# Decoder trunk: last two inner column tiles by rows, a join queued behind the first half's hi part, last products in halves

## The chip, the cores and the metric

One Trainium2 chip, one of its cores. The time is the device time of one execution in microseconds (us), the median over runs. Before the change it is 1212.53 us (three runs, 1212.32 to 1212.62).

The core's engines are named as in the profile: PE (TensorE, matrix products), PEld (its weight load), ACT (ScalarE), DVE (VectorE), POOL (GpSimd) and SP (SyncE, which issues most DMAs here). "t" is the token block: 256 tokens are two blocks of 128, t=0 and t=1.

## What is computed

Two layers, each of three residual steps with a layer norm behind it; the change touches the two feed-forward steps (four in all, at `i` = 0 and 2) and every layer norm.

```python
def _swiglu(x, w1, w3, w2):
    return (jax.nn.silu(x @ w1) * (x @ w3)) @ w2
...
for l in range(DEPTH):                                   # DEPTH = 2
    h = _swiglu(x, ffn_w1[l, 0], ffn_w3[l, 0], ffn_w2[l, 0])
    x = _layernorm(ALPHA * x + 0.5 * h, ln_g[l, 0], ln_b[l, 0])
    h = _mixer(x, l, ...)                                # projections, gating unit, attention, merge
    x = _layernorm(ALPHA * x + h, ln_g[l, 1], ln_b[l, 1])
    h = _swiglu(x, ffn_w1[l, 1], ffn_w3[l, 1], ffn_w2[l, 1])
    x = _layernorm(ALPHA * x + 0.5 * h, ln_g[l, 2], ln_b[l, 2])
```

x is 256 x 1024 in float32, the inner width of a feed-forward step is 2816 = 22 tiles of 128 columns.

## The kernel before

**Arithmetic.** Every float32 operand is split into a hi part (rounded to the PE's fp32r type by an ACT copy) and a lo part (source minus hi, by DVE). A product is three matmuls: hi x hi, lo x hi and hi x lo. All weights stream in as 1 MB pieces `raw` (ring of 4) by SP, are split by ACT and DVE into `whi` and `wlo` (rings of 8 each), and are used once.

**First feed-forward matrix.** Inner tiles 0 to 19 are five blocks of four tiles, computed *by rows*: x is the stationary operand, 512 weight columns move, and each block's two products (w1 and w3) land in a PSUM bank with tokens on partitions (`gemm_first`, `gemm_b2`, `gemm_rows`). `front` takes SiLU on ACT, the product with the w3 bank on DVE, writes the result as two 16-bit planes (`planes`, ACT), and SP turns them with two DMA transposes per block (L704). `columns` (L681 to L693) joins the turned planes on ACT and splits the result for the second matrix. Inner tiles 20 and 21 are computed *by columns* in `gemm_a2` (L275 to L302): the weights are stationary; for each of four weight tiles eight matmuls of 512 columns move x hi and x lo together (L283), then, for each tile, eight matmuls of 256 columns bring in the weights' lo part (L290). Each tile then takes one ACT copy (L291) and one DVE addition (L293), and each pair SiLU and a product (L721, L722). The result comes out inner-width first and needs no turning.

**Second feed-forward matrix.** Tiles 4 to 13 go through five rounds of a seven-product scheme (`SQ`, `stream_s`); the pairs 0-1, 2-3 and 14 to 21 are plain products (`PQ`). After the first round comes the first plain pair, after the second round the second, then the rounds go on alone. The last four plain pairs are *held* until the end, so that the four output blocks (t, c), c being the 512-column half, finish one after the other and the layer norm of t=0 can begin while PE is still at t=1.

**Layer norm into the next step** (`Norm`). `part_s` adds a finished block to the residual on DVE and accumulates its sum, `finish_s` takes the sum of squares on ACT (L553), the reciprocal root on DVE and normalises 512 columns at a time (L556). The second 512 columns go through planes (L184) and a DMA transpose (`send`); the first 512 are turned by PE (L633). `turn(t, h)` then brings half h of the normalised rows to the stationary form of the next step: for h = 0 out of PSUM, for h = 1 by a *join* of the turned planes (ACT, L628), then four ACT operations with scale and shift (L638), the hi part on ACT and the lo part on DVE (`split`, L233 and L234). The next step's PE work starts with t=0, c=0, for which half h = 0 must be there. Weight splits of the next step run on ACT and DVE at the same time (L174, L178, L207, L216, L227, L229).

**The last norm** (`part`, `finish`) has no next step: each block is added to the residual on DVE (L567), its statistics taken per 256 columns (L572), and for the last token block the columns below 768 are multiplied by the gain (L574) and finished through PE (L588, L592), the last 256 on DVE; six DMAs write the result.

**Order of work.** PE's order is the order in which the program is written, with turns of side tasks slotted in by a running beat counter. The other engines' order is set by a list scheduler when the program is built: by priority (`soon()` raises it by two chunks) among what its model of the time calls ready. `behind(ins)` queues an instruction after `ins` on the same engine and adds no wait of its own. Each engine's queue runs strictly in that order on the chip.

Of the kernel before, what the change touches and what calls it, by code (L numbers as in the profile page):

```python
# [58 lines left out]
def trunk(ctx, tc, x, xT, w13a, w13b, w2s, w2p, wb, wqk, wa, wbr, wo, gateb, sgug, sgub, sguwT, sgubias, lam, diffg,  # L59
# [89 lines left out]
    latest, added, emptied, silu, turned_by, early = [None, None], [None], [None], [None], [None], [None]  # L149
# [5 lines left out]
    def stream(src, width=CH, sub=HC, lent=(), after=(None, None)):  # L155
# [7 lines left out]
        for o in range(0, width, HC):  # L163
# [7 lines left out]
            for p, (h, w) in zip(range(0, HC, sub), at):  # L171
                r = raw[:, o + p : o + p + sub]
                with behind(latest[0] if o // HC in lent else early[0] or latest[0]):
                    copied = A.activation(h, r, AF.Copy)  # L174
                if o // HC in lent:
                    early[0] = copied.ins
                with behind(after[o // HC] or latest[1]):
                    V.tensor_tensor(out=w, in0=r, in1=h.bitcast(F32), op=ALU.subtract)  # L178
# [330 lines left out]
    class Norm:  # L509
# [6 lines left out]
        def __init__(self, l, i, scale, eps, after, last=False):  # L516
            self.scale, self.eps, self.last, self.done = scale, eps, last, set()
            self.ends, self.xlo, self.pre, self.sent = [None] * NT, {}, None, {}
# [103 lines left out]
        def turn(self, t, h):  # L622
            self.done.add((t, h))
            xf = s512("xf")
            if h:
                b = xf
                with soon():
                    A.activation(xf.bitcast(U16).rearrange("p (k w) -> p k w", w=2),  # L628
                                 self.sent[t].rearrange("p (w k) -> p k w", w=2), AF.Copy)
            else:  # L630
                b = side_bank()
                for k in range(4):
                    PE.transpose(b[:, k * P : (k + 1) * P], self.y[t][:, k * P : (k + 1) * P], ident)  # L633
# [7 lines left out]
            self.xlo[t, h] = last[1]  # L641
# [9 lines left out]
    def ffn(l, f, i, norm, following=None):  # L651
# [29 lines left out]
        def columns(ins):  # L681
            while waiting:
                k0, tt = waiting.pop(0)
                h = tmp.tile([P, 2, 512], F32, tag="columns", name=name("columns"), bufs=1)
                to = h.bitcast(U16).rearrange("p q (k u t w) -> p (q k) u t w", k=2, u=2, w=2)
                for t in range(NT):
                    with behind(ins):
                        A.activation(to[:, :, t], tt[:, t].bitcast(U16).rearrange("p (w c t) -> p c t w", w=2, c=FB),
                                     AF.Copy)
                for j in range(2):  # L690
# [19 lines left out]

        if norm is None:
# [28 lines left out]
        for n, q in enumerate(SQ):  # L740
# [4 lines left out]
            if n < len(PQ) - HELD:  # L745
                plain_pair(n)
        u, v = s512("u"), s512("v")
# [13 lines left out]
        for t in range(NT):  # L761
            for c in range(2):
                for ps, o, n in ends[t, c]:
                    for q in PQ[-HELD:]:
                        rows_p(ps, t, q, held[q, c], hh, hl, o, n, stop=q == PQ[-1])
                    if not last:
                        ln.part_s(t, c, ps)
                        continue
                    for o in ((0, 256) if last and (t, c) == (1, 1) else (0,)):
                        ln.part(t, c * 512 + o, ps[:, o : o + 256] if o or last and (t, c) == (1, 1) else ps, 1.0)  # L770
# [244 lines left out]
def _layout(i):  # L1015
# [32 lines left out]
    o["w13a"] = c(np.stack([cols(w1[..., nb:]), cols(w3[..., nb:])], axis=4)).reshape(L, 2, FT - FR, P, CH)  # L1048
# [52 lines left out]
```

## Time and profile before

| | us |
|---|---|
| median of 3 runs | 1212.53 (1212.32 to 1212.62) |
| profiled execution, its own time | 1213.05 |
| span of its instructions | 1211.3 |
| PE busy | 1203.7 (99% of the span) |
| PEld / DVE / ACT / POOL busy | 1011.3 / 942.9 / 857.4 / 91.1 |
| granted PE clock | 1.00 |
| DMA | 212 GB/s mean |

How to read it: an engine's rows are instructions with start and duration in us from the span's start. A matmul's duration is modelled and overlaps the next one, so PE's pace is read from starts: a run of n matmuls in the chain of waits has n times the spacing. "x2" in a row means two instructions merged in one row. In brackets stands the idle time before an instruction and what ended it.

### The profile page before, as it was taken

How to read it: one execution, taken by the hardware profiler on the slowest of the kernel's cores; microseconds unless marked ns; L12 is line 12 of the kernel's file. 1: busy time of each engine (PE TensorE's matmuls, PEld its weight loads, DVE VectorE, ACT ScalarE, POOL GpSimd, SP SyncE). 2: the span in 40 equal slices, each digit the busy share in tenths (PEclk: the TensorE clock that was granted, in tenths of full speed). 3: DMA queues.
4: the chain of work that ended last, by engine and by line, in shares of the span. 5: the costliest groups of instructions: out<-in, count | busy, mean ns of one | idle time of the engine just before them, and what ended most of it. 6: DMA issues, size and time to landing. Idle time of an engine off the chain costs nothing.

```text
span 1211.3 us, 16542 instructions
## 1 busy us (share of the span) xinstructions
PE 1203.7 (99%) x5961; PEld 1011.3 (83%) x5961; DVE 942.9 (78%) x1540; ACT 857.4 (71%) x1384; POOL 91.1 (8%) x184
## 2 busy tenths in 40 slices
PE   9999999999999999999999999999999999999998
PEld 8888888888888878888888888888888888888886
DVE  6658998885696876579985679989766877757797
ACT  7677677679865595776776776776898556867761
POOL 0100000233300000000000000003331000000000
PEclk9999999999999999999999999999999999999999
DMA  8985665655764658665668665766648456677551
GB/s 321 323 261 174 211 249 208 227 177 166 232 227 164 217 178 282 191 192 218 229 216 270 195 176 207 254 223 199 213 139 273 176 174 217 201 259 210 184 202 47
DMA packets 101346, 257.00 MB, mean 212 GB/s; under 512 B 66528, under 2 KB 67600, under 8 KB 74640
## 3 DMA queue, kind: packets, MB, share of 16 engines
q1 hardware_dynamic: 97296, 243.03, 59.9%
q0 software_dynamic: 3536, 12.13, 3.2%
q8 instruction: 46, 0.75, 0.3%
q10 hardware_dynamic: 432, 0.79, 0.2%
q14 instruction: 36, 0.29, 0.1%
HBM read 235.47 MB, written 1.05 MB: 195 GB/s over the span
## 4 chain that ended last, share of the span: by engine, by line
PE 91%; DVE 4%; ACT 3%; issue 1%; DMA 0%; SPq 0%; POOL 0%; DVEq 0%; ACTq 0%; POOLq 0%
PE bank L271 35%; PE sbank L271 24%; PE bank L283 16%; PE bank L290 8%; PE sbank L283 2%; PE bank L446 2%; PE sbank L290 1%; PE sbank L829 1%; DVE wlo L178 1%; PE sbank L961 1%; ACT pp L839 0%; DVE nwa L248 0%; ACT xf L638 0%; ACT whi L174 0%; PE sbank L878 0%
## 5 line engine op out<-in xcount | busy, mean ns | idle before, releaser
L178 DVE TENSOR_TENSOR wlo<-raw,whi 128x1024 fp32r<-128x1024 f32 (+1 forms) x396 | 436.6, 1125 | 144.5 <-ACT whi L174 113.9
L174 ACT ACTIVATE whi<-raw 128x1024 fp32r<-128x1024 f32 (+1 forms) x396 | 372.9, 971 | 124.4 <-PE bank L283 43.2
L271 PE MATMUL bank<-whi,x 128*128 128x512 f32 x840 | 263.3, 390 | 0.0
L271 PEld LDWEIGHTS bank<-whi,x 128*128 128x128 f32 x840 | 157.7, 188 | 32.9 <-DVE gz L293 0.2
L271 PE MATMUL bank<-wlo,x 128*128 128x512 f32 x420 | 163.5, 389 | 0.0
L271 PE MATMUL sbank<-whi,x 128*128 128x512 f32 x512 | 158.9, 389 | 0.0
L283 PE MATMUL bank<-x,whi 128*128 128x512 f32 x640 | 156.0, 394 | 0.0
L283 PEld LDWEIGHTS bank<-x,whi 128*128 128x128 f32 x640 | 117.1, 188 | 26.3 <-issue 2.3
L271 PEld LDWEIGHTS sbank<-whi,x 128*128 128x128 f32 x512 | 96.1, 188 | 20.0
L353 ACT ACTIVATE shi<-raw 128x1024 fp32r<-128x1024 f32 (+1 forms) x80 | 73.4, 946 | 51.7 <-DVE raw L368 26.4
L271 PE MATMUL sbank<-wlo,x 128*128 128x512 f32 x256 | 99.6, 389 | 0.0
L355 DVE TENSOR_TENSOR slo<-raw,shi 128x1024 fp32r<-128x1024 f32 (+1 forms) x80 | 85.4, 1088 | 14.1 <-ACT shi L353 13.3
L271 PEld LDWEIGHTS bank<-wlo,x 128*128 128x128 f32 x420 | 78.9, 188 | 16.0
L290 PE MATMUL bank<-x,wlo 128*128 128x256 f32 x640 | 85.9, 285 | 0.0
L290 PEld LDWEIGHTS bank<-x,wlo 128*128 128x128 f32 x640 | 81.6, 191 | 2.2
L291 ACT ACTIVATE r<-bank 128x256 f32<-128x256 f32 x112 | 41.6, 377 | 24.0 <-PE bank L290 24.0
L271 PEld LDWEIGHTS sbank<-wlo,x 128*128 128x128 f32 x256 | 48.1, 188 | 9.9
L271 PE MATMUL sbank<-whi,hhi 128*128 128x512 f32 x144 | 56.3, 391 | 0.0
L271 PE MATMUL sbank<-whi,hlo 128*128 128x512 f32 x144 | 56.1, 390 | 0.0
L271 PE MATMUL sbank<-wlo,hhi 128*128 128x512 f32 x144 | 56.0, 389 | 0.0
L506 POOL DMA_DIRECT2D bc<-in_lng x6 | 3.2, 530 | 696.2 <-DVE bc L505 696.2
L702 ACT ACTIVATE planes<-silu 128x1024 uint16<-128x1024 uint16 x40 | 42.0, 1053 | 7.3 <-DVE silu L701 6.2
(247 smaller groups left out, 1999.1 us busy)
## 6 DMA issues: line engine op xcount, KB each, us to landing
raw<-in_w13b SPq DMA_DIRECT2D x76, 1024.0 KB, 5.4
raw<-in_w2p SPq DMA_DIRECT2D x24, 1024.0 KB, 4.9
raw<-in_wa SPq DMA_DIRECT2D x24, 1024.0 KB, 5.4
raw<-in_w2s SPq DMA_DIRECT2D x20, 1024.0 KB, 4.9
raw<-in_wb SPq DMA_DIRECT2D x16, 1024.0 KB, 5.3
raw<-in_wqk SPq DMA_DIRECT2D x16, 1024.0 KB, 4.8
raw<-in_wbr SPq DMA_DIRECT2D x16, 1024.0 KB, 4.9
raw<-in_w13a SPq DMA_DIRECT2D x8, 1024.0 KB, 4.8
```

Of the source, the lines that this page charges most:

```text
L174: copied = A.activation(h, r, AF.Copy)
L178: V.tensor_tensor(out=w, in0=r, in1=h.bitcast(F32), op=ALU.subtract)
L271: PE.matmul(ps, xx, w, start=start and n == 0, stop=stop and n == 2)
L283: PE.matmul(b[-1], hi[:, k * P : (k + 1) * P], xc(k), start=k == 0, stop=False)
L290: PE.matmul(b[n][:, :T], lo[:, k * P : (k + 1) * P], xc(k)[:, :T], start=False, stop=k == KT - 1)
L291: emptied[0] = A.activation(r[:, s], b[n][:, T:], AF.Copy, scale=scale).ins
L353: A.activation(h, r, AF.Copy)
L355: V.tensor_tensor(out=w, in0=r, in1=h.bitcast(F32), op=ALU.subtract)
L446: PE.matmul(ps[t][m], x[:, j, o + t * P : o + (t + 1) * P], y, start=k0 + j == 0 and o == 0 and y is hi, stop=k0 + j == KT - 1 and y is lo)
L702: A.activation(pk.rearrange("p (w k) -> p w k", w=2), s.bitcast(U16).rearrange("p (k w) -> p w k", w=2), AF.Copy)
L829: PE.matmul(banks[m][:, j * nk : (j + 1) * nk], rows(qT, m, j, t * P, P), rows(kT, m, j, 0, nk), start=True, stop=True)
L961: PE.matmul(b[:, j * T + t * P : j * T + (t + 1) * P], vg[t][:, g // 4, s], wsT[g // 4][:, s], start=True, stop=True)
```

## The change

Three parts:

1. Tiles 20 and 21 are computed by rows too (`narrow`): w1 and w3 of both tiles are one 512-wide moving operand, two banks, one per t, each with w1 in its first and w3 in its second 256 columns. SiLU, product, planes and a DMA transpose follow per t, at half of `front`'s width. The join and split of the block before (`columns`) come after t=1's SiLU; those of the two tiles come after the second plain pair's weight split (`copied`). The weights' layout in memory follows.
2. In `turn`, the join of half h = 1 is queued behind the hi part of half h = 0 of the same t.
3. In the last feed-forward step the last output block, (t, c) = (1, 1), is multiplied in two halves of 256 columns. The first half adds on to the block's bank; the second has a new bank of its own, and what the old bank has for it is added to the residual on DVE while PE works at the second half. The first half's addition, statistics and gain come ahead of the second half's end.

```diff
@@ turn
-                with soon():
+                with soon(), behind(self.xhi[t]):
                     A.activation(xf.bitcast(U16).rearrange("p (k w) -> p k w", w=2),
                                  self.sent[t].rearrange("p (w k) -> p k w", w=2), AF.Copy)
...
-            self.xlo[t, h] = last[1]
+            self.xhi[t], self.xlo[t, h] = last
@@ ffn
+        def narrow():
+
+            tt = act.tile([P, 2, 512], F32, tag="val", name=name("turned"), bufs=2)
+            ps = [side_bank() for _ in range(NT)]
+            for c in range(2):
+                for n, piece in enumerate(stream(w13a[l, f, :, c * CH : (c + 1) * CH])):
+                    for t in range(NT):
+                        rows_b(ps[t], t, 4 * c + 2 * n, piece, xh, xl, KT)
+            for t in range(NT):
+                s, pk = t512("silu"), s512("planes")[:, :T].bitcast(U16)
+                silu[0] = A.activation(s[:, :T], ps[t][:, :T], AF.Silu).ins
+                V.tensor_tensor(out=s[:, :T], in0=s[:, :T], in1=ps[t][:, T:], op=ALU.mult)
+                planes(pk, s[:, :T])
+                nc.sync.dma_start_transpose(out=tt[:, t, :T].bitcast(U16).rearrange("p (c t) -> p c t", c=4), in_=pk)
+            columns(silu[0])
+            waiting.append((FR, tt))
+            return s
...
-        for j in range(FR, FT, 2):
-            qa = s512("qa")
-            for m, z in gemm_a2([w13a[l, f, j - FR + m] for m in range(2)], both, lambda m: t512("silu"), bank=side_bank):
-                s = z[:, :T]
-                silu[0] = A.activation(s, s, AF.Silu).ins
-                V.tensor_tensor(out=qa[:, m * T : (m + 1) * T], in0=s, in1=z[:, T:], op=ALU.mult)
-                columns(silu[0])
-            keep((j, j + 1), qa)
-        ln = Norm(l, i, 2.0 * ALPHA, 4.0 * EPS, qa[:, :1], last)
+        s = narrow()
+        ln = Norm(l, i, 2.0 * ALPHA, 4.0 * EPS, s[:, :1], last)
...
             if n < len(PQ) - HELD:
                 plain_pair(n)
+            if n == len(PQ) - HELD - 1:
+                columns(copied[0])
...
-                for ps, o, n in ends[t, c]:
...
+                (ps, _, _), = ends[t, c]
+                if last and (t, c) == (1, 1):
+                    y, right = ln.y[t][:, 768:], bank()
+                    for b, o, opens in ((ps, 0, False), (right, 256, True)):
+                        for q in PQ[-HELD:]:
+                            rows_p(b[:, :T], t, q, held[q, c], hh, hl, o, 256, stop=q == PQ[-1],
+                                   start=opens and q == PQ[-HELD])
+                        ln.part(t, 512 + o, b[:, :T], 1.0)
+                        if not opens:
+                            V.tensor_tensor(out=y, in0=y, in1=ps[:, T:], op=ALU.add)
+                    continue
```

`columns` takes a block of two tiles as well (`nq`: one pair and half the planes instead of two pairs), and `stream` notes its last hi copy in `copied`.

More of the change, by code (lines that the diff above doesn't have):

```diff
@@ L762, in ffn @@
             for c in range(2):
-                for ps, o, n in ends[t, c]:
[L764 to L770, printed above, removed]
+                (ps, _, _), = ends[t, c]
[9 more added lines that the diff above has]
+                    continue
+                for q in PQ[-HELD:]:
+                    rows_p(ps, t, q, held[q, c], hh, hl, 0, 512, stop=q == PQ[-1])
+                if last:
+                    ln.part(t, c * 512, ps, 1.0)
+                else:
+                    ln.part_s(t, c, ps)
             (ln.finish if last else ln.finish_s)(t, ((2, 1.5), (2, 1))[t])
```

20 lines of the change are left out of this document (11 added, 9 removed).

## The prediction

> **What bounds the kernel now.** I read the page first: where the span goes, and which engine carries the chain that ended last.
>
> ```profile
> span 1211.3 us, 16542 instructions
> ...
> PE 1203.7 (99%) x5961; PEld 1011.3 (83%) x5961; DVE 942.9 (78%) x1540; ACT 857.4 (71%) x1384; POOL 91.1 (8%) x184
> ...
> PE 91%; DVE 4%; ACT 3%; issue 1%; DMA 0%; SPq 0%; POOL 0%; DVEq 0%; ACTq 0%; POOLq 0%
> ```
>
> PE is the bound nearly everywhere. Time can only come from three places: cheaper matmuls, the few spots where PE waits, and the tail behind the last matmul. So I read the chain of waits next, in order of time, for the pace of PE around the columns that change form.
>
> ```profile
> 92.98 21.76 PE bank L271 x96
> 114.74 7.25 PE sbank L283 x32
> 121.99 3.83 PE sbank L290 x32
> 125.82 2.75 PE bank L271 x12
> ```
>
> Columns: start, duration, what. A block by rows is 96 matmuls of 512 columns in 21.76 us, 0.2267 us each. The column form starts exactly when the block before it ends (92.98 + 21.76 = 114.74), so nothing is waited for there; its 32 matmuls of 256 columns take 3.83 us, 0.1197 each, more than half of 0.2267. Then the waits, PE's alone: total, times, longest.
>
> ```profile
> PE sbank L633 <- DVE xtok L556: 0.8, 2, 0.4
> PE bank L271 <- DVE x L234: 0.5, 3, 0.2
> ```
>
> These two are the norm transitions: three times PE waits for the lo part of the first normed half, twice for rows to turn. There are five transitions: the three times are those out of a feed-forward step, the two those out of a mixer.
>
> **Part 1, tiles 20 and 21 by rows.** Removed per feed-forward step: 32 x 512 and 32 x 256 columns, 7.25 + 3.83 = 11.08 us, and 0.03 of restart behind it (2.75 against 12 x 0.2267 = 2.72). Added: 8 k-tiles x 2 token blocks x 3 matmuls = 48 of 512 columns, 48 x 0.2267 = 10.88 us. The columns streamed are the same; what goes is the surplus of the short matmuls. Saving 0.23 per step, 0.92 over four; low end 0.2 each, 0.8.
>
> The Trainium skill speaks against a surplus of this size: its page "TensorE: Matmul & The Clock Gate", section "Back-to-back issue gap", gives an isolated warm gap of N/2.4 + 2.5 ns, so 109 ns for 256 columns and 216 for 512; by that a split costs 2.5 ns per extra matmul, part 1 would give an estimated 0.04 per step, part 3 would cost 0.06, and the sum below would be 2.7 instead of 3.1. The trace disagrees, with 119.7 and 226.7 ns.
>
> On the other engines: four ACT copies and four DVE additions of 256 columns go, four in number on each; two planes operations, two joins at half width and two DMA transposes per step come. The block before has the same kind of work at full width inside a 21.76 us stage in which PE never waits, so I cost it at nothing. Queues: SP now has two transposes that wait for the planes, and the next weight load stands behind them if the scheduler puts it there; ACT has two joins and a hi split behind the second plain pair's weight split, with the third round's splits queued behind. Who would suffer is DVE, which is full there:
>
> ```profile
> 146.25:160.53 14.28, 14.28 (x64) 11.83 (x64) 14.00 (x15) 9.68 (x11) 0.00 (x0) 1.00 0.55 197
> ```
>
> In this stretch (PE, PEld, DVE, ACT) DVE works 14.00 of 14.28 us. But the change takes four additions off it shortly before, so it enters the stretch ahead rather than behind. Part 1: -0.92.
>
> **Part 2, the join behind the hi part.** First a transition out of a feed-forward step: PE, ACT, DVE (start, duration, instruction).
>
> ```profile
> 182.87 0.39 PE L271 MATMUL bank<-llo,x 128*128 128x512 f32 x1
> 183.44 0.73 PE L271 MATMUL bank<-lhi,x 128*128 128x512 f32 x2 [0.18 <-DVE x L234]
> 184.01 0.39 PE L271 MATMUL bank<-llo,x 128*128 128x512 f32 x1
> ...
> 189.92 0.60 PE L633 MATMUL sbank<-ident,xtok 128*128 128x128 f32 x4
> ```
> ```profile
> 179.38 1.49 ACT L638 ACTIVATE xf<-sbank,ln_b,ln_g 128x128 f32<-128x128 f32 x4
> 180.76 1.19 ACT L628 ACTIVATE xf<-sent 128x1024 uint16<-128x1024 uint16 x1
> 181.84 0.63 ACT L233 ACTIVATE x<-xf 128x512 fp32r<-128x512 f32 x1
> ```
> ```profile
> 182.09 0.69 DVE L178 TENSOR_TENSOR wlo<-raw,whi 128x512 fp32r<-128x512 f32 x1
> 182.69 0.69 DVE L234 TENSOR_TENSOR x<-xf,x 128x512 fp32r<-128x512 f32 x1
> ...
> 188.48 1.00 DVE L556 TENSOR_SCALAR xtok<-xtok,mv,nwy 128x512 f32<-128x512 f32 x2
> ```
>
> From 182.87 to 184.01 PE starts three matmuls, 0.68 at its pace; it takes 1.14, so 0.46 is lost. It waits for the lo part (182.69 + 0.69 = 183.38), which stands on DVE right behind a weight split, and for whose hi part (181.84) ACT first ran the join of the other half (180.76, to the next start 1.08). With the join behind it the hi part comes 1.08 earlier or, if the scheduler puts a weight split of about 0.5 into the freed slot, about 0.55 earlier; in both cases it is there before 182.09, and the lo part can have the weight split's slot: it ends at 182.78, PE needs it at 182.87 + 0.23 = 183.10, and the wait is gone. Behind `behind` nothing else waits: the join and the half that hangs on it come at most 0.5 to 1.1 later, and PE needs that half only 24 matmuls, 5.4 us, after the first. DVE's queue order is fixed when the program is built, so the gain needs the scheduler to see the hi part earlier too; a hi part earlier by one ACT operation should move the lo part by at least one DVE operation, since it has priority. Next late are PE's transposes of t=1 (189.92): their rows are normalised at 188.48 + 1.00 = 189.48, and 0.46 earlier PE would stand there at 189.46 and wait a little. I take 0.40 of 0.46, three times: 1.20; ends 0 and 3 x 0.46 = 1.38.
>
> Out of a mixer the same order does something else:
>
> ```profile
> 426.14 0.50 PE L271 MATMUL bank<-lhi,x 128*128 128x512 f32 x1
> ...
> 427.44 0.39 PE L271 MATMUL bank<-llo,x 128*128 128x512 f32 x1
> ...
> 433.89 0.66 PE L633 MATMUL sbank<-ident,xtok 128*128 128x128 f32 x4 [0.39 <-DVE xtok L556]
> ```
> ```profile
> 424.38 1.18 ACT L628 ACTIVATE xf<-sent 128x1024 uint16<-128x1024 uint16 x1
> 425.46 0.63 ACT L233 ACTIVATE x<-xf 128x512 fp32r<-128x512 f32 x1
> ...
> 428.56 1.14 ACT L553 ACTIVATE sq<-xtok,mv 128x1024 bf16<-128x1024 f32 x1
> ```
> ```profile
> 426.12 0.69 DVE L234 TENSOR_TENSOR x<-xf,x 128x512 fp32r<-128x512 f32 x1 [2.05 <-ACT x L233]
> ```
>
> Here DVE itself stood idle 2.05 us for the hi part, so the lo part surely comes earlier, and the 0.39 that PE loses from 426.14 to 427.44 (1.30 for four matmuls, 0.91 at pace) goes. But PE then only arrives earlier at the transposes (433.89), for which it waits 0.39 already and which hang on t=1's sum of squares (ACT, 428.56). That operation has no idle in front of it: it comes when ACT's queue comes to it. If it stays at 428.56, the gain is 0. If the scheduler, seeing the lo part and so the sums earlier, puts it ahead of one ACT operation of 0.5 us, the gain is 0.5, at most 0.39 + 0.39 = 0.78. If one more weight split gets in front of it, 0.5 is lost. Both ends lie close; I take 0.25, twice: 0.50; ends -1.0 and 1.56.
>
> **Part 3, the last block in halves.** DVE behind the last matmul:
>
> ```profile
> 1203.13 0.75 DVE L567 TENSOR_TENSOR xtok<-xtok,sbank 128x256 f32<-128x256 f32 x2 [2.38 <-PE sbank L271]
> 1203.80 0.74 DVE L572 BATCH_NORM_STATS2 st<-xtok 128x6 f32<-128x256 f32 x2
> 1204.46 0.41 DVE L574 TENSOR_TENSOR xtok<-xtok,bc 128x256 f32<-128x256 f32 x1
> 1204.78 0.26 DVE L579 BATCH_NORM_AGGREGATE mv<-st 128x2 f32<-128x24 f32 x1
> ```
>
> Between the first addition (1203.13) and the aggregate (1204.78) lie five operations in 1.65 us, 0.33 each. Three of them, the first half's addition, statistics and gain, move under the second half's matmuls (24 x 0.1197 = 2.9 us; with the new addition of the old bank's rest four operations, 1.3 us, so they are hidden). Left are two that depend on each other, so rather 0.41 to 0.45 each than 0.33: 0.9. Saved 0.75, at most 0.99. Added on PE: 48 x 0.1197 - 24 x 0.2267 = 0.30, wholly on the path. Net 0.45; ends 0.15 (if two new banks and the changed order cost PE as much again, 0.3) and 0.75. Everything behind the aggregate keeps its length.
>
> **The sum.** 0.92 + 1.20 + 0.50 + 0.45 = 3.07. The profiled execution's own time, 1213.05 (span 1211.3 and 1.75 around it), becomes 1209.98. It lies 0.52 above the median of the runs, 1212.53, and I take the runs' scale: 1212.53 - 3.07 = 1209.46, rounded 1209.5. What a measurement of this kernel can tell from no change is about 0.2%, 2.4 us: faster begins below 1210.1.
>
> **Rivals.** *The lo part stays where it is on DVE.* The weight split at 182.09 keeps its slot because the scheduler's time for the hi part is still later. Then the 1.20 fails and 0.92 + 0.50 + 0.45 = 1.87 is left: 1210.7, no measurable change. For it: DVE ran without a gap ahead of 182.69, so nothing on the chip forces a new order. Against: the three waits look alike, so one order decides all three, and the lo part has priority. Chance 0.22.
>
> *The later join costs as much as the earlier hi part gives,* at the mixers above all: the sum of squares slips by one ACT operation, 0.5 each, and 0.92 + 1.20 - 1.0 + 0.45 = 1.57 is left: 1211.0, no measurable change. For it: 428.56 has no slack. Against: its input comes earlier with the lo part, so it can as well move forward. Chance 0.15, small misses of several terms included.
>
> *Slower: SP's new transposes hold a weight load back.*
>
> ```profile
> 116.06 2.60 SPq L704 DMA_TRANSPOSE turned<-planes  x2
> ```
> ```profile
> 126.08 0.34 SPq L344 DMA_DIRECT2D raw<-in_w2s  x1
> ```
>
> The planes of the two tiles are there, by an estimate of SiLU, product and planes at 0.4 to 0.5 each (256 columns took 0.41 at L574), about 1.5 us after the two tiles' matmuls end at 125.8, at 127.3. If the load now at 126.08 is queued behind their two transposes (up to 2.60, as at 116.06), it goes at about 130. DVE in the rounds behind has 14.28 - 14.00 = 0.28 us to spare plus the 1.3 of four removed additions; from 1.6 us of starvation on, every further one is a us of PE, four times. At 3 us it is 4 x 1.4 = 5.6 against 3.07: 1215.1. For it: SP's queue is in order, and DVE is full there. Against: the full-width transposes at 116.06 stand in the same place of the block before and PE did not wait. Chance 0.06.
>
> **How the numbers follow.** The forecast has 0.57. Faster is the forecast alone, 0.57; the two middle rivals are no change, 0.37; the last is slower, 0.06. The range goes from 0.92 + 1.38 + 1.56 + 0.75 = 4.6 saved, rarely all at once, so 1207.9, to the middle rivals with the low ends of parts 1 and 3 (0.8 + 0 - 0.5 + 0.15 = 0.45), 1212.1.
>
> **What the changed profile would show.** Part 1: behind the last full block 48 matmuls of 512 columns in 10.88 us, at L271, and the next round starting 0.23 earlier. Part 2: no wait of PE for L234, 0.57 between two starts gone at three places; ACT with the hi part ahead of the join at all five; at the mixers the sum of squares tells which way it went. Part 3: the aggregate 0.9 behind the last addition's start. I am wrong if the three waits stand, if PE waits anew in the rounds behind the two tiles (L353 or L355 as what ended it), or if the transposes out of the mixers come later than now.

## The result and the profile after

The changed kernel takes 1219.26 us (median of 6 runs, 1217.05 to 1222.44) against 1212.70 (6 runs, 1212.32 to 1213.84). The ratio is 1.0053, 95% interval [1.0043, 1.0064]; the ratios here are taken over all runs, so they are not quite the quotients of the medians beside them. It is slower by 0.5%, where 0.3% faster was forecast. Its profiled execution took 1222.44 us, the longest of the six and 9.4 more than the one of before, so what the profile shows place by place adds up to more than the 6.6 us between the medians. One execution each of e2, e3 and e10 below was a slow one (2018.92, 6922.22 and 2092.35 us) and is left out of the numbers given for them.

From the page of the changed kernel, the span, the engines' busy time and the chain by engine:

```profile
span 1220.7 us, 16437 instructions
...
PE 1207.2 (99%) x5921; PEld 1010.9 (83%) x5921; DVE 937.9 (77%) x1525; ACT 861.2 (71%) x1384; POOL 90.2 (7%) x184
...
PE 62%; issue 20%; ACT 6%; DVE 6%; DMA 3%; POOL 2%; SPq 1%; DVEq 0%; POOLq 0%; ACTq 0%
```

PE stays 99% busy, since a matmul that is issued late is still counted. The chain tells more, but its shares have to be read with care: PE's falls from 91% to 62%, yet most of what it loses are two stretches of "issue", 77.23 and 135.75 us long, that end at 1014 and 1154 us. There the trail goes back along POOL's queue, which is idle ahead of the DMA issues of the norm's gain (`bc<-in_lng`), while PE works on. What counts is that such a DMA has entered the chain in the last feed-forward step. The chain of waits at the columns that changed form:

```profile
93.17 21.76 PE bank L272 x96
114.93 10.88 PE sbank L272 x48
125.81 2.72 PE bank L272 x12
```

10.88 us against 7.25 + 3.83, and the next round without a restart: part 1 does on PE what it promised. The waits of PE (total, times, longest):

```profile
PE sbank L853 <- ACT aT L889: 2.3, 2, 1.1
PE sbank L634 <- DVE xtok L557: 1.8, 3, 0.8
PE bank L272 <- DVE slo L356: 1.7, 2, 0.9
PE sbank L887 <- DVE pp L872: 1.6, 2, 1.3
```

The wait for the lo part (L234, now L235) is gone, as forecast. Three that were not there have come: two in attention (L853, L887), one in the rounds (`slo`, L356). Differences of the same matmuls' starts in the two traces say where the 9.40 us of span came from:

| place | us |
|---|---|
| first feed-forward step, its rounds included | +0.28 |
| transitions out of three feed-forward steps | +0.38, -0.28, -0.22 |
| attention of layer 0, of layer 1 | +1.87, +3.87 |
| rows in the second, third and fourth step | -0.20, -0.15, -0.24 |
| rounds of the fourth step | +4.46 |
| last block and tail | -0.38 |
| the two transitions out of a mixer | 0 |

**The rounds of the last step.** The changed kernel's DVE, then its ACT, then ACT of the kernel before, in order of time:

```profile
1156.25 0.69 DVE L235 TENSOR_TENSOR hlo<-columns,hhi 128x512 fp32r<-128x512 f32 x1 [2.45 <-ACT hhi L234]
1158.29 0.69 DVE L235 TENSOR_TENSOR hlo<-columns,hhi 128x512 fp32r<-128x512 f32 x1 [1.34 <-ACT hhi L234]
1161.01 2.36 DVE L356 TENSOR_TENSOR slo<-raw,shi 128x1024 fp32r<-128x1024 f32 x2 [2.03 <-ACT shi L354]
```
```profile
1156.24 1.28 ACT L532 ACT_TABLE_LOAD   x1
1157.54 0.20 ACT L532 ACTIVATE first<-mask 128x1 f32<-128x1 f32 x1
1157.64 0.62 ACT L234 ACTIVATE hhi<-columns 128x512 fp32r<-128x512 f32 x1
1158.97 1.06 ACT L526 ACTIVATE bc<-bc 128x1024 f32<-128x1024 f32 x1 [0.71 <-DMA bc<-in_lng]
1159.94 1.99 ACT L354 ACTIVATE shi<-raw 128x1024 fp32r<-128x1024 f32 x2
```
```profile
1150.05 1.28 ACT L531 ACT_TABLE_LOAD   x1
...
1152.29 1.06 ACT L353 ACTIVATE shi<-raw 128x1024 fp32r<-128x1024 f32 x1 [0.21 <-DVE raw L368]
...
1155.60 1.06 ACT L525 ACTIVATE bc<-bc 128x1024 f32<-128x1024 f32 x1 [0.35 <-DMA bc<-in_lng]
```

DVE stands idle for 2.45 + 1.34 + 2.03 = 5.8 us. This is ahead of the rounds in which, in the first step, it had 0.28 us to spare. ACT is the reason: the square root's table load, and the scaling of the norm's gain (L526), which waits for its own DMA, stand in ACT's queue ahead of the second round's hi splits (1159.94). In the kernel before, the table load stood there too, but such a split ran at 1152.29, ahead of the gain scaling (1155.60).

**Attention, last head pair.** DVE of the changed kernel, and of the kernel before:

```profile
268.98 0.69 DVE L833 TENSOR_TENSOR qk<-qk,swap 128x512 f32<-128x512 f32 x1 [1.46 <-POOL swap L829]
...
270.11 1.40 DVE L872 SCALAR_TENSOR_TENSOR pp<-pp,c,pp 128x256 f32<-128x256 f32 x4
```
```profile
267.99 1.40 DVE L848 SCALAR_TENSOR_TENSOR pp<-pp,c,pp 128x256 f32<-128x256 f32 x4
269.31 0.68 DVE L809 TENSOR_TENSOR qk<-qk,swap 128x512 f32<-128x512 f32 x1
```

The softmax difference `pp`, for which PE waits, now stands behind the last rotary addition, which waits for POOL. Nothing in the diff touches these lines.

**Out of a mixer.** PE and ACT of the changed kernel:

```profile
435.28 0.39 PE L272 MATMUL bank<-whi,x 128*128 128x512 f32 x1
436.44 0.66 PE L634 MATMUL sbank<-ident,xtok 128*128 128x128 f32 x4 [0.77 <-DVE xtok L557]
```
```profile
427.46 0.63 ACT L234 ACTIVATE x<-xf 128x512 fp32r<-128x512 f32 x1
427.98 1.19 ACT L629 ACTIVATE xf<-sent 128x1024 uint16<-128x1024 uint16 x1
...
431.12 1.14 ACT L554 ACTIVATE sq<-xtok,mv 128x1024 bf16<-128x1024 f32 x1
```

The join stands behind the hi part, the 0.39 of PE's wait is gone, and the wait at the transposes grows by the same 0.39, to 0.77. **The tail**, DVE of the changed kernel:

```profile
1213.25 0.42 DVE L568 TENSOR_TENSOR xtok<-xtok,bank 128x256 f32<-128x256 f32 x1 [1.04 <-PE bank L272]
1213.70 0.43 DVE L573 BATCH_NORM_STATS2 st<-xtok 128x6 f32<-128x256 f32 x1
1214.16 0.26 DVE L580 BATCH_NORM_AGGREGATE mv<-st 128x2 f32<-128x24 f32 x1
```

From the start of the last addition to that of the aggregate it is 0.91 us, where before it was 1.65 from the first addition.

### The profile page after: what moved, and what is told of

It reads as the page before. It is cut to its first block, busy times and chain, and to the rows that moved or that the text cites. A ratio compares the mean times of both kernels' runs of the same rounds, so it can differ in the third digit from the quotient of the medians.

```text
span 1220.7 us, 16437 instructions
## 1 busy us (share of the span) xinstructions
PE 1207.2 (99%) x5921; PEld 1010.9 (83%) x5921; DVE 937.9 (77%) x1525; ACT 861.2 (71%) x1384; POOL 90.2 (7%) x184
## 4 chain that ended last, share of the span: by engine, by line
PE 62%; issue 20%; ACT 6%; DVE 6%; DMA 3%; POOL 2%; SPq 1%; DVEq 0%; POOLq 0%; ACTq 0%
PE bank L272 24%; PE sbank L272 22%; PE bank L284 9%; PE bank L291 4%; PE bank L447 2%; ACT whi L174 1%; DVE wlo L179 1%; ACT xf L639 1%; DMA bc<-in_lng 1%; DVE slo L356 1%; DMA swap<-z 1%; ACT pp L863 1%; POOL nwa L263 1%; DVE pp L872 1%; SPq L825 1%
## 5 line engine op out<-in xcount | busy, mean ns | idle before, releaser
L272 PE MATMUL sbank<-whi,x 128*128 128x512 f32 x640 | 199.1, 389 | 0.0
L272 PEld LDWEIGHTS sbank<-whi,x 128*128 128x128 f32 x640 | 120.2, 188 | 24.9
L272 PE MATMUL sbank<-wlo,x 128*128 128x512 f32 x320 | 124.6, 389 | 0.0
L356 DVE TENSOR_TENSOR slo<-raw,shi 128x1024 fp32r<-128x1024 f32 (+1 forms) x80 | 85.6, 1088 | 25.4 <-ACT shi L354 24.2
L272 PEld LDWEIGHTS sbank<-wlo,x 128*128 128x128 f32 x320 | 60.1, 188 | 12.5
L272 PE MATMUL sbank<-whi,hhi 128*128 128x512 f32 (+1 forms) x144 | 55.5, 386 | 0.0
L272 PE MATMUL sbank<-whi,hlo 128*128 128x512 f32 (+1 forms) x144 | 55.3, 384 | 0.0
L272 PE MATMUL sbank<-wlo,hhi 128*128 128x512 f32 (+1 forms) x144 | 55.2, 384 | 0.0
L690 ACT ACTIVATE columns<-turned 128x1024 uint16<-128x1024 uint16 (+1 forms) x48 | 50.7, 1090 | 1.3 <-DMA turned<-planes 1.2
```

Source lines behind the costliest of these rows:

```text
L272: PE.matmul(ps, xx, w, start=start and n == 0, stop=stop and n == 2)
L690: A.activation(to[:, :, t], tt[:, t, : nq * T].bitcast(U16).rearrange("p (w c t) -> p c t w", w=2, c=2 * nq), AF.Copy)
```

## The experiments

**Each part alone.** Of the three kernels e1, e2 and e3, the first keeps only `narrow` with its layout and the moved `columns`, the second only this edit, the third only the halved last block:

```diff
-                with soon():
+                with soon(), behind(self.xhi[t]):
```

> Part 1 alone (tiles 20 and 21 by rows in all four steps; no join edit, no halves). Theory A (each part costs where the changed order of its own engines queues): PE's 0.2 per step is there, 4 x 0.2 = 0.8 saved, but in the last step ACT's queue holds the weight splits of the first rounds behind the late joins, the sqrt table load and the gain's scaling, DVE starves and PE loses about 4.5: 1212.7 - 0.8 + 4.5 = about 1216. The fourth head pair of the attention stands as before. Rival B (the two more DMA transposes and the shifted weight loads delay the swaps' landing in the attention): this kernel carries nearly all of the loss, about 1219, with waits at the transposes of the attention. Rival C (part 1 alone is what was forecast): 1211.8.

> Part 2 alone (join of half 1 behind the hi part of half 0). Theory A: three waits at the first normed half go, most of it given back at the transposes of t=1, about 0.5 net; but the list scheduler puts the rotary addition of the last head pair ahead of the softmax difference on DVE in both layers, so PE waits 1.9 and 3.9 there: 1212.7 - 0.5 + 5.8 = 1218, at least 1215. Rival B (landing of the swaps, caused by part 1's DMAs): no loss here, 1212.2.

> Part 3 alone. Theory A and the forecast agree: the tail is 0.4 to 0.5 shorter, 1212.2 to 1212.3, everything before the last block in the same order and at the same times. A rival that puts part of the loss here (PE at another pace after the new bank) gives 1213 or more.

| kernel | median (range) | ratio [95%] |
|---|---|---|
| e1, part 1 | 1217.23 (1216.34 to 1221.77) | 1.0045 [1.0033, 1.0058] |
| e2, part 2 | 1215.74 (1214.47 to 1216.58) | 1.0024 [1.0015, 1.0033] |
| e3, part 3 | 1212.69 (1212.00 to 1213.84) | 1.0001 [0.9992, 1.0010] |

The kernel before stood at 1212.76. Part 1 loses 4.5 us and part 2 3.0; together that is more than the 6.6 of the whole change, so the parts do not simply add. In their traces, against the kernel before: e1 gains 0.15 to 0.25 in the second to fourth steps, loses 2.67 in the last step's rounds, 0.59 at the first transition, 0.93 and 0.35 in attention. e2 gains 0.22, 0.21 and 0.19 at the three transitions, nothing at the mixers, and loses 1.27 and 1.18 in attention. e3 gains 0.44 in the tail, too little for its interval. The waits of PE in e1 name the rounds' loss with the same row as in the changed kernel, 1.7 us for `slo` (L356), twice.

**The order on DVE.** e2's join, and the last head pair's rotary addition queued behind the softmax difference, where it stood before (`lessed` is the last `pp` instruction):

```diff
-                with behind(None if last else added[0]):
+                with behind(lessed[0] if last else added[0]):
```

> Part 2 alone, and in the attention the rotary addition of the last head pair is queued behind the softmax difference of the pair before, as the kernel before has it. Theory A: the attention's loss goes for the most part, 1212.2 to 1213.5. If the order of these two on DVE isn't the cause (the ACT order, the POOL chain or the landing of the swaps is), the time is that of part 2 alone, about 1216 to 1218.

1213.65 us (1213.19 to 1214.09), ratio 1.0007 [0.9998, 1.0015]: 2.1 us less than e2. Its DVE has the old order:

```profile
266.17 2.34 DVE L884 SCALAR_TENSOR_TENSOR pp<-pp,c,pp 128x256 f32<-128x256 f32 x4
268.44 0.68 DVE L845 TENSOR_TENSOR qk<-qk,swap 128x512 f32<-128x512 f32 x1
```

Attention loses 0.27 and 0.45 now instead of 1.27 and 1.18. So the join's loss is mainly that exchange: one added order edge changed the built queues far away, and two instructions there were exchanged. That it did so through the scheduler's model of the time is the likely way; no run shows it. The difference of 2.1 us holds a little of a third cause, the packets below, as well.

**The last step's ACT queue, four kernels that did not win the time back.** In e5 (part 1 alone) the table load and the gain scaling move behind the second plain pair's weight split; e6 keeps the columns form in the last step only; e7 is e5 with the join and split of the block before issued ahead of the two tiles' SiLU; e8 adds the halves to e7.

```diff
-                A.activation(self.g, self.g, AF.Copy, scale=-0.5)
...
+        def late(self, ins):
+            with behind(ins):
+                A.activation(sm("first", 1), mask[:, :1], AF.Sqrt)
+                A.activation(self.g, self.g, AF.Copy, scale=-0.5)
...
                 columns(copied[0])
+                if last:
+                    ln.late(copied[0])
```

> Part 1 alone, and in the last step the sqrt table load and the scaling of the gain wait on ACT until behind the second plain pair's weight split. Theory A (in the last step ACT's queue holds the second round's hi splits behind the table load and the gain, which waits for its DMA; DVE starves): most of part 1's loss goes, from 1217.2 to 1212 to 1213; DVE's idle of 5.6 before its second round shrinks to about 3, as in the other steps. Rival B (the late joins and the two tiles' own planes are what starves DVE, in the last step as in the others): 1216 or more. Rival C (the swaps of the attention or the weight loads come later because of the added transposes): 1217 as before.

> Part 1 alone, in the first three feed-forward steps; the last one by columns as before. Theory A: the saving of 0.2 per step is left and the last step's stall is gone: 1212.0 to 1212.6. If the loss were spread over the steps (rival B) or lay in the attention (rival C): three quarters of it, or all, stays: 1216.

> As the kernel with the late gain, and the join of the block before the two tiles is issued ahead of the two tiles' SiLU, not behind it. Theory A: DVE's remaining idle of about 2.7 per step at the start of the second round shrinks as well; PE has no wait left there, so the gain in time is small: 1211.8 to 1212.5. If the starvation in the first three steps costs nothing, the time is that of the kernel with the late gain alone.

> Parts 1 and 3 with both repairs, without the join edit. If the parts add up: the time of the kernel without halves less 0.4, 1211.4 to 1212.1, that is 0.05 to 0.1 per cent faster than the kernel before, at the edge of what five rounds can tell.

| kernel | median (range) | ratio [95%] |
|---|---|---|
| e5 | 1216.53 (1215.01 to 1217.94) | 1.0028 [1.0018, 1.0039] |
| e6 | 1214.56 (1211.24 to 1217.47) | 1.0018 [1.0010, 1.0026] |
| e7 | 1220.88 (1218.55 to 1223.71) | 1.0068 [1.0055, 1.0081] |
| e8 | 1221.91 (1216.94 to 1224.52) | 1.0070 [1.0054, 1.0086] |

None of the four came into its forecast. e5's place was still ahead of hi splits of the rounds (the table load at 1159.18, splits at 1162.06): its last step loses 2.1 us. It loses 0.85 and 2.9 in the two attentions as well, and e7 and e8 lose 2.6 and 3.5 in layer 1's; the packets below explain that. e6 has no loss in the last step, but 0.96 in layer 0's attention, where its queues have the kernel before's order, and a spread of 6 us. e7 shows the same in-order queue at another place, its ACT in the first step:

```profile
139.03 0.69 ACT L692 ACTIVATE columns<-turned 128x512 uint16<-128x512 uint16 x1 [5.57 <-DMA turned<-planes]
139.63 0.62 ACT L354 ACTIVATE shi<-raw 128x512 fp32r<-128x512 f32 x1
```

The two tiles' `columns` now waits 5.57 us for its DMA transpose, and the hi split behind it waits too; PE loses 4.3 us there. The runs give the slack as well. DVE's idle time from 11 us ahead of the rounds to their end, and PE's stall in them: 1.3 and 0.06 (before), 2.7 and 0.03, 3.5 and 0.2, 3.8 and 0.5 (e6, first step), 4.8 and 2.1 (e5), 5.6 and 2.7 (e1), 7.5 and 4.3 (e7). Up to some 3 us cost nothing, and more costs about one for one. This is a rough rule of these traces: idle time behind the last split for the rounds does not count, as in e9's last step below, where 1.6 us of DVE's idle time lie there and PE's stall is 0.03.

**Behind the last round, and the join where no attention follows.** e9 is parts 1 and 3 with `late` behind the last round's hi split; e10 adds the join in the norm from layer 0 into layer 1; e11 is the whole change with `late` there and the pinned order.

```diff
             beat(1.75)
+            if last and n == NS - 1:
+                ln.late(cuts[0])
```

> Parts 1 and 3 without the join; in the last feed-forward step the square-root table load and the gain scaling leave the first two rounds and stand in ACT's queue behind the splits of the last round. Theory A (in the last step ACT's queue, held by table load, gain scaling and the held products' column copies, keeps the hi parts of the rounds from DVE): DVE's idle time in the last step falls from 5.6 us to at most 3.5 us and PE's stall there from 2.7 us to at most 0.3 us; the time is the 1217.2 us of part 1 alone less 2.5 and less 0.4 for the halves, about 1214.3 us. Rival (the rows form itself starves the rounds, by SP's two new transposes ahead of the weight loads): PE's stall stays above 2 us and the time at 1216.5 us or more.

> The kernel of the run before, and the join queued behind the hi part only in the norm that leads from layer 0's last feed-forward step into layer 1's first, where no rotary pairs follow. If the join's loss is only the order of DVE's queue in attention: the transition gains 0.2 us, attention is as without the join, the time is 0.1 to 0.3 us under the run before. If any change of the queues ahead of attention disturbs it: 0.5 us or more over the run before.

> The whole change with two orders put back: the last rotary addition behind the softmax difference, and the table load and gain scaling behind the last round's splits. If these two orders carry the loss: the last step loses 0.3 us at most and attention about 1 us in both layers together, against 0.6 us for rows, 0.6 us at three transitions and 0.4 us of the tail: 1212.5 to 1214 us. If the loss lies in what the change computes and not in the orders: 1216 us or more.

e9: 1213.48 (1212.14 to 1214.80), ratio 1.0007 [0.9998, 1.0016]. e10: 1214.55 (1213.13 to 1217.23), 1.0016 [1.0007, 1.0025]. e11: 1214.91 (1213.34 to 1217.66), 1.0018 [1.0010, 1.0027]. e9's ACT in the last step:

```profile
1150.54 1.04 ACT L354 ACTIVATE shi<-raw 128x1024 fp32r<-128x1024 f32 x1
1151.49 0.62 ACT L234 ACTIVATE hhi<-columns 128x512 fp32r<-128x512 f32 x1
1152.01 1.05 ACT L354 ACTIVATE shi<-raw 128x1024 fp32r<-128x1024 f32 x1
```

The hi splits run at once, and PE's stall in the last step's rounds is 0.03 us instead of 2.72; 3.75 us of median are back, 0.44 of them for the halves. No run moves the table load without the gain scaling, so which of the two weighs more is open. The rival fell: SP's two new transposes per step are still there. At their new place, in front of the held weight splits, the two cost about 0.8 us (e13, which moves them further, has no loss there). e10 gained 0.2 at that transition in the profile, yet its median is 1.1 above e9's; why is open. e11 came out 0.9 us above its range: attention still lost 0.56 and 1.32.

**What moves attention.** Part 1 leaves attention's queues as they were, and still every kernel so far with it and without attention's join edit lost 0.8 to 1.3 us in layer 0. The records of the DMA packets (a packet is one piece of a DMA transfer) show one thing that moves: single packets of 16 KB on queue 8, of which the profile page of the kernel before has 46, 0.75 MB, under the kind "instruction". PE has 5961 matmuls and as many weight loads; 11,922 over 46 packets is 259 instructions each, so they are taken for PE's code. Part 1 removes 16 matmuls and 16 weight loads per step, and each packet comes later by that much. The swap of a rotary pair, four small DMAs that SP issues and POOL waits for, is where it matters, above all the seventh pair's. Four kernels without part 1 have the packet of layer 0 at 254.2 to 254.5 us; the nine with it, up to e11, at 256.0 to 260.8. In layer 1 the packet of the kernel before lies at 851.74, ahead of the seventh swap, and in the changed kernel at 859.42, inside it. SP and POOL there, before and after:

```profile
853.06 2.41 SPq L801 DMA_DIRECT2D swap<-z  x4
```
```profile
856.99 1.28 POOL L805 TENSOR_TENSOR swap<-swap,sin_t 128x512 f32<-128x512 f32 x1 [9.12 <-DMA swap<-z]
```
```profile
856.41 2.41 SPq L825 DMA_DIRECT2D swap<-z  x4
```
```profile
862.26 1.28 POOL L829 TENSOR_TENSOR swap<-swap,sin_t 128x512 f32<-128x512 f32 x1 [12.72 <-DMA swap<-z]
```

From SP's first issue to POOL's start it is 3.93 us before and 5.85 after. All 19 traces sort this way, with two seventh swaps each: where no packet of queue 8 starts between the two, they are 3.93 to 4.19 us apart (18 swaps), and where one does, 4.41 to 6.13 (20 swaps). e5, e7 and e8, which lost 2.6 to 3.5 us in layer 1's attention, have a packet there (5.3 to 6.1 us); e1, e6, e9, e10 and e13 have none, and lost at most 0.35. Of the next four kernels, e12, e14 and e15 move the packets by the warm-up alone.

```diff
-    for _ in range(WARM):
-        PE.matmul(b[:, :P], warm, warm, start=True, stop=True)
+    for _ in range(21):
+        PE.matmul(b[:, :224], warm[:, :P], warm[:, :224], start=True, stop=True)
```

(e12, with a `warm` of 224 columns; e14 and e15 have 85 matmuls of 48 columns there.) e13 is parts 1 and 3 with `late` behind the last held splits, e14 is e13 with the longer warm-up, e15 the kernel before with it.

> The kernel before with 21 warm-up matmuls of 224 columns in place of 37 of 128: the same warm-up time, 16 weight loads and 16 matmuls fewer ahead of everything, as many as one feed-forward step by rows has fewer. Nothing else moves. Theory B (the 16 KB code fetch on DMA queue 8, 1.3 to 1.5 us on one DMA engine, comes after every 20 to 30 us of PE's instructions; with fewer PE instructions it comes some 2.5 us later in attention, and there it holds back two packets of the seventh rotary pair's swap): the fetch at 254.5 us comes at 256.5 to 257.5 us, the swap lands 3.4 to 4.2 us after its last issue instead of 2.1, layer 0's attention loses 0.7 to 1.1 us, the time is 1213.3 to 1214 us. Rival (the swaps land late for another reason, the weight loads that part 1 moves): no loss, 1212.6 us.

> Parts 1 and 3 without the join, table load and gain scaling behind the last held splits, where only the last two norms follow: theory A gives the last step without either stall, so the 1213.5 us of the kernel with them behind the last round's splits less the 1.0 us that PE waits there for the held lo parts: 1212.4 us. If that wait is not the table load's: 1213.5 us.

> The run before with 85 warm-up matmuls of 48 columns in place of 37 of 128: 96 PE instructions more ahead of everything, so that the code fetch of layer 1's attention comes back from 860 to about 852.5 us, where it is in the kernel before, and that of layer 0 moves from 256 to about 248.5 us, between two swaps. Theory B: layer 0's attention gets its 1.0 us back and the time is 1211.0 to 1211.6 us, under the kernel before. Rival: as the run before.

> The kernel before with the same 85 warm-up matmuls, as a control: the fetch of layer 0's attention comes at about 247 us instead of 254.5 and that of layer 1's at about 844 instead of 851.7, neither between the issue of the seventh pair's swap and its landing. Theory B: within 0.4 us of the kernel before, so that what the run ahead of this one gains is not the warm-up's. Rival (the longer warm-up helps or hurts by itself): 0.5 us or more off.

| kernel | median (range) | ratio [95%] | packet in layer 0, 1 at | attention |
|---|---|---|---|---|
| before | 1212.80 (1212.12 to 1213.81) | | 254.5, 851.7 | |
| e12 | 1214.06 (1213.38 to 1214.71) | 1.0009 [1.0001, 1.0018] | 257.1, 854.3 | +0.72, +0.24 |
| e13 | 1212.61 (1211.97 to 1216.67) | 1.0004 [0.9995, 1.0012] | 257.2, 860.0 | +1.29, +0.29 |
| e14 | 1211.55 (1210.89 to 1214.30) | 0.9996 [0.9987, 1.0005] | 251.7, 850.8 | -0.87, 0 |
| e15 | 1213.23 (1212.85 to 1215.62) | 1.0009 [1.0001, 1.0018] | 250.5, 843.3 | -0.81, 0 |

e12 changes the warm-up alone, and layer 0's attention loses 0.72 us, where part 1 alone loses 0.93. (It loses 0.3 at the start as well.) Its DMA queues between 257 and 258 us (queue, packets, MB, share of 16 engines), then SP and POOL:

```profile
q8 instruction: 1, 0.02, 6.8%
```
```profile
254.17 2.41 SPq L801 DMA_DIRECT2D swap<-z  x4
```
```profile
259.52 1.29 POOL L805 TENSOR_TENSOR swap<-swap,sin_t 128x512 f32<-128x512 f32 x1 [10.67 <-DMA swap<-z]
```

One packet takes 6.8% of 16 engine-us, 1.09 us of one DMA engine. SP is done with the four issues at 256.58, and POOL gets the swap 2.94 us later. The same rows of e14, whose packet came ahead of the swap:

```profile
253.02 2.41 SPq L829 DMA_DIRECT2D swap<-z  x4
```
```profile
257.13 1.28 POOL L833 TENSOR_TENSOR swap<-swap,sin_t 128x512 f32<-128x512 f32 x1 [9.43 <-DVE wlo L179]
```

Done at 255.43, and POOL starts 1.70 us later. And the kernel before, whose packet lay between 254 and 255 us:

```profile
q8 instruction: 1, 0.02, 9.1%
```
```profile
253.38 3.54 SPq L801 DMA_DIRECT2D swap<-z  x4
```
```profile
258.43 1.29 POOL L805 TENSOR_TENSOR swap<-swap,sin_t 128x512 f32<-128x512 f32 x1 [10.25 <-DMA swap<-z]
```

It pays too: its issues took 3.54 us instead of 2.41. From SP's first issue to POOL's start it is 5.05 us before, 5.35 in e12, 4.11 in e14. So of e12's 0.72 us this swap explains 0.30. The rest came earlier: another packet, at 238.54, met the fifth pair's swap, and POOL started 4.42 us after its first issue (238.32), against 3.95 before, where the packet came at 237.27, ahead of the issue (237.97). The packet records show how. Each swap transfer ends with 16 packets of 4 bytes, taken here for its semaphore's 16 increments, one of each DMA engine. Of the swap's last transfer in e14 the 16 start between 256.31 and 256.54. In e12 fifteen start between 257.47 and 257.69, and the sixteenth at 258.57, 0.88 later; the 16 KB packet had ended at 258.18. In e9 it is fifteen from 256.45 to 256.69 and one at 257.77, 1.08 later, behind two 2 KB packets, the first of which starts as the 16 KB packet ends (257.36).

e15 was to be a neutral control and was not: it gained 0.81 in attention, but in its profiled execution lost 1.7 us at the start (below), and 1.1 where a packet met another small transfer. Its SP, its DMA queue between 1023 and 1024 us, and its ACT's wait:

```profile
1020.92 1.24 SPq L189 DMA_TRANSPOSE sent<-planes  x1
```
```profile
q8 instruction: 1, 0.02, 6.8%
```
```profile
ACT xf L628 <- DMA sent<-planes: 1.0, 1, 1.0
```

The turned rows land 4.4 us after the issue instead of 2.7, and ACT, and PE behind it, wait 1.0. That is the mechanism at another transfer.

e13 came out where theory A put it (1212.4 forecast), and e14 gains 1.06 over it: 1211.55 is 1.25 us under the kernel before by the medians, though its interval takes in no change. The comparison flatters the change: of e14's 1.9 us in the profile, 0.87 are a shorter attention, and e15 shows that the same warm-up gives the kernel before 0.81 there.

**The changed kernel with the causes taken away.** e16 is the changed kernel with 85 warm-up matmuls; e17 has the pinned order and `late` behind the held splits as well.

> The changed kernel with 85 warm-up matmuls of 48 columns in place of 37 of 128, so that the code fetch comes about 7.5 us earlier in attention, as in e14. Theory: the fetch's part of attention's loss goes (about 2 of 5.7 us in the profile, more in layer 1 than in layer 0, since there the fetch at 859.4 us is in the middle of the swap); what is left is the order of DVE's queue (about 2.3 us) and the last step (2.7 to 4.5 us): 1216.5 to 1218 us against 1219.3. If the fetch has no part in it: 1219 us or more.

> The whole change with all three causes put right: the last rotary addition behind the softmax difference, table load and gain scaling behind the last held splits, and the longer warm-up. If the three causes are all there is: the 1211.55 us of e14 less 0.6 us for the lo part's wait at three transitions plus 0.3 to 0.9 us that the pinned join left in attention in e4: 1211.2 to 1212 us. If something else in the join costs beside parts 1 and 3: 1213 us or more.

e16: 1217.73 (5 runs, 1215.54 to 1219.42), ratio 1.0035 [1.0022, 1.0049]. e17: 1213.73 (1211.54 to 1214.91), ratio 1.0005 [0.9997, 1.0014]. e16 came into its range. In its profiled execution attention loses 0.68 and 1.54 instead of 1.87 and 3.87, 0.8 are lost behind layer 0's attention, and 1.9 at the start. e17's profiled execution loses 1.7 there, gains 0.26, 0.29 and 0.26 at the three transitions, and no place but layer 1's attention (0.86) loses any more. Its median lies 1.7 us above its range, in the range for which its expectation named "something else in the join". Its eleven runs fall into two groups, four from 1211.54 to 1212.53 and seven from 1213.70 to 1214.91. The profiled one (1213.73) is of the second, so the loss at the start, which e14's profiled execution does not have, may be what parts them; the other runs have no trace that could show it. So the three causes are not shown to be all.

## Why the prediction was wrong

**The step that failed is part 1's paragraph on the other engines: "so I cost it at nothing".** The changed profile loses 4.46 us in the last step's rounds and 5.74 in attention, where the forecast had no loss at all. The step had two holes.

The first is ACT. The prediction found the right place (DVE full in the rounds) and named ACT's new items in the queue, but then looked at DVE's load alone: "the change takes four additions off it shortly before, so it enters the stretch ahead rather than behind". DVE cannot use that lead, since its hi parts come from ACT, and in the last step ACT also has a 1.28 us table load and a scaling that waits for a DMA, which part 1's new items brought ahead of the hi splits. e9 and e13 show it: with those two moved, e1's stall of 2.7 us is 0.03. The rival that ended slower had DVE starving in the rounds, but through SP's weight loads, in all four steps, and with 0.06; the queue was ACT's and the step the last. Its bound of 1.6 us was too tight: about 3 us are free.

The second is the code. "The columns streamed are the same; what goes is the surplus" counted PE's time but not its instructions. 32 fewer per step shift each 16 KB packet. In layer 0 one met the seventh swap before and meets it at a dearer moment after (5.05 and 6.02 us to POOL's start), and in layer 1 one now falls on it (3.93 and 5.85); e12 shows 0.72 in layer 0 from the shift alone, and e16 has 3.5 us less loss in attention than the changed kernel. No row that the prediction quoted could have priced it, but the profile page has the queue, and the sum had no term for transfers that move without being touched.

**Part 2** failed in its size and in what it left out. The wait of PE for the lo part did go, as forecast. Of 3 x 0.40 the join alone brought 0.62, 0.81 in e17: PE then waits at the transposes, which the prediction named as "next late" and priced at 0.06 each. At the mixers the 0.50 was 0: the sum of squares did not move ahead, and the 0.39 turned up in the next wait, the case that the text gave as "the gain is 0". "Behind `behind` nothing else waits" left out the build: with the edge the list scheduler exchanged `pp` and `qk`, for about 2 us (e2 against e4).

**Part 3** was right: 0.45 forecast, 0.44 in e3's profile, with 0.30 added on PE and 0.73 saved behind it; 0.38 in the changed kernel.

**Part 1 on PE** was right too: 0.23 forecast, 0.15 to 0.25 measured where nothing else moved.

What stays open: why the spread of kernels with part 1 is so wide (the packet's place explains a part, and varies from 256.0 to 257.6 us among traces of kernels that are alike up to there), the 0.4 to 0.6 that most of those without the join lose at the first transition, e10, and e17. That the packets are PE's code is inferred from their count and from e12, not seen, and so is that a held-up packet and the 16 KB packet share a DMA engine: the records name no engine.

## What to carry to other kernels

An operation that is moved in an engine's queue must be priced by whoever is queued behind it, down to the engine that is full: here ACT's late items starved DVE, and DVE starved PE. In a program whose order a list scheduler makes, compare the built queues everywhere, since one added edge can exchange two instructions in another phase. And a change in the bottleneck engine's instruction count moves its code fetches, which can hold back small transfers that something waits for; a few idle instructions at the start tell whether a loss is of that kind.

## What the runs showed of the hardware

**The code packet.** It takes 0.88 to 2.23 us in these traces, 0.96 at the median, on what is taken for one of the 16 DMA engines. A seventh swap that it meets reaches POOL 0.2 to 2.2 us later than one that it does not meet, and a DMA transpose that it met landed in 4.4 us instead of 2.7. The Trainium skill's page "Runtime: NRT & Kernel Launch", section "Instruction fetch mechanics", states refills in blocks of 16 KiB, 256 instructions, and a cost that is mostly hidden. The block agrees with 259 here. That the cost is hidden agrees for PE, none of whose waits in the kernel before (3.5 us in all) is put down to a packet; it does not hold for the swap and the transpose that met one.

**PE's clock.** In the changed kernel's last rounds two stalls of about a us, 1183.6 to 1186.7, were followed by matmuls spaced 0.43 us. Its stretches (PE, PEld, DVE, ACT, POOL, then the granted clock):

```profile
1183.00:1187.00 4.00, 2.31 (x8) 1.17 (x8) 3.97 (x6) 3.61 (x5) 0.00 (x0) 1.00 0.15 64
1187.00:1191.00 4.00, 4.00 (x12) 3.09 (x12) 4.00 (x4) 4.00 (x5) 0.00 (x0) 0.57 0.76 262
```

The granted clock falls to 0.57 in the second. That is 8 spacings of 0.43 instead of 0.23, 1.6 of the 4.46 us. e1 has the same two stalls (1.41 and 1.16 between starts) without it. So in this case two stalls of that length were followed by the lower clock once and once not. Kernels with 85 warm-up matmuls of 48 columns show the like at the start: in e15's profiled execution nine spacings from the second matmul on are 0.43 us, where the kernel before has one of 0.39, 1.7 us lost; e16 and e17 have the same, and e14 none. The trace's clock records fit: the first, of a full clock, stands at 9.90 us in e15, at 6.17 in the kernel before and at 4.15 in e14.
